# Key and value jobs in turn, eight slots for weights, a second U tile and new scheduler durations in a hybrid attention and DeltaNet layer

## The chip, the core and the metric

One core of a Trainium2 chip runs the whole layer as one program. The metric is the device time of that core in microseconds, from runs of the compiled kernel. The engines are PE (TensorE), DVE (VectorE), ACT (ScalarE), POOL (GpSimd) and SP (SyncE, which issues the DMAs here). All matrices are in float32 at the interface.

## The reference

One decoder layer over 1024 tokens of width 2048, and a final RMSNorm.

```python
h = rms_norm(x, norm_w)
proj = einsum('btd,dc->btc', h, w_in)          # 2048 -> 8208 columns
# group A, 8 heads: differential attention
attn = softmax(q1 k1^T * scale + bias) - lam * softmax(q2 k2^T * scale + bias)
o_da = rms_norm(attn @ v, subln_w) * (1 - lambda_init) * silu(gate)
# group B, 8 heads of 128: gated DeltaNet
q, k, v = silu(causal_depthwise_conv(qkv, conv_w))
o_gdn = gated_delta_rule_chunked(l2norm(q), l2norm(k), v, g, beta)   # chunks of 64
o_gdn = rms_norm(o_gdn, gdn_norm_w) * silu(z)
out = rms_norm(x + concat(o_da, o_gdn) @ w_out, final_norm_w)
```

## The kernel before, in words

**The input projection.** It is cut into jobs. One job makes two blocks of 128 columns for all 1024 tokens, by a scheme with seven products for every four quarter blocks (in the manner of Strassen). Its four quarter weights A11, A12, A21 and A22 are 128 x 1024 float32, 512 KB each, loaded from w_in in rows of 128 columns. Three more operands (S1 to S4, some in place) are sums of these. One product is 24 matmuls of 128x128 by 128x512: eight blocks deep, and three passes, since each float32 operand is split into a float16 value and a float16 remainder (whi and wlo for the weights; B11h, B11l and so on for the activations, made once at the start). There are 32 jobs, in this order (lines 1567 to 1597): four of DeltaNet keys, four of attention values, then for every pair of heads one of gates and two of queries and keys, three of z, eight of DeltaNet queries and values (one per head), and one last of z.

**The weights task** (`weights`, from line 700) runs one step for each product of the job at hand. A step splits one operand (ACT writes whi, then DVE or POOL writes wlo) and does a part of the preparation of the next job: load the four quarters (steps 0 to 3), square each on ACT (steps 1 to 4, each in the step after its load), add the squares up by a small matmul into the PSUM tile `side` (step 5), derive a power-of-two scale for each half, scale the quarters on ACT, and form S1 to S4 on POOL. The raw tiles are a ring of six: one job allocates six slots (A11, A21, S1, A12, A22, S2), so that a quarter of the next job takes the slot of the same quarter of this one.

**Collecting.** Each product is read out of PSUM (two `prod` tiles) and added into the tiles q, U, V and o (`collect`). Of each there is one; only in the second and the fourth job a tile U1 of another pool stands in for U. When a tile is complete, a consumer does what the columns are for. `ev_tile` holds a new use back until the consumers of the last are done.

**What follows.** Each pair of key jobs' heads goes through convolution, Gram matrix and decay (`key_head`), in a lane of its own. After the fourth key job's heads, `inverse` inverts all 128 triangular blocks of 64 on DVE (62 dependent pairs of operations on the tiles tmp and A), merges them on PE, and then starts `attention`: 128 units (8 heads, 8 query blocks, 2 maps). A DeltaNet query or value job's consumer waits for the last head of attention, as it takes over the memory (`head_state`). After the last job and the last scan come 28 groups of four products of the output projection, whose operands are sums and splits made on ACT and on DVE or POOL.

**What sets the order.** Nothing is ordered at run time. `Planner` (from line 175) holds lanes, each a list of generators of instructions; again and again it issues the instruction or DMA that could start earliest by its own clock, made of `Op.cost`, of the delays in `HOP`, and for DMAs (`start`, line 287) of 0.475 us on the queue, 0.65 us, the bytes over 360 GB/s and 0.8 us until others see it. A `Choice` may go to DVE or POOL, whichever ends first, with a lean. During attention a margin (`plan.margin`) keeps its units in step with the products. On the chip each engine runs its instructions in the order thus written, and waits at the first whose operands are not ready. All of them are recorded on line 273, and DMAs on 303, so the rows are told apart by tile names.

Of the kernel before, what the change touches and what calls it, by code (L numbers as in the profile page):

```python
# [23 lines left out]
D = 2048  # L24
H = 8
# [99 lines left out]
class Choice:  # L125
    """The same computation on either of two engines, the second preferred by so many microseconds."""
# [14 lines left out]
class Copy:  # L141
    """A DMA that is still to be issued."""
# [8 lines left out]
class Lane:  # L151
    """Tasks (generators of instructions and conditions) that are issued one after the other."""
# [21 lines left out]

class Planner:
    """Orders the instructions of several lanes by an estimate of when each can start."""

    def __init__(self, tc, lanes):
        self.tc, self.nc = tc, tc.nc
        self.free = dict(pe=0.0, act=0.0, dve=0.0, pool=0.0, queue=0.0, dma=0.0)  # L180
# [6 lines left out]
        self.now = 0.0  # L187
        self.margin = lambda: 0.8
# [98 lines left out]
    def start(self, d):  # L287
# [8 lines left out]
        size = free_len(d.out) * d.out.shape[0] * 4  # L296
# [3 lines left out]
        self.wr[o] = {"dma": max(t1 + 0.8, self.wr.get(o, {}).get("dma", 0.0))}  # L300
        rd = self.rd.setdefault(i, {})
        rd["dma"] = max(t1 + 0.8, rd.get("dma", 0.0))
# [36 lines left out]
class Pool:  # L339
    """A tile pool whose slots the planner follows."""  # L340
# [29 lines left out]
def hybrid_trunk(ctx: ExitStack, tc: tile.TileContext, a, out):  # L370
# [275 lines left out]
    # (operands of the narrow product, the rows of its weights, the column group of the sum)  # L646
# [52 lines left out]

    def weights():  # L700
        cur = None
        for j in range(len(jobs) + 1):
            nxt = {"j": j} if j < len(jobs) else None
            cols = jobs[j][0] if nxt is not None else None

            def load(n):
                c, g = {"A11": (0, 0), "A12": (0, 1), "A21": (1, 0), "A22": (1, 1)}[n]
                t = nxt[n] = wp.tile([P, NH, P], F32, "raw", 6)
                dma(t, w_v[:, g * NH:(g + 1) * NH, cols[c]:cols[c] + P])

            def square(n, k):
                return act.activation(junk(D // 2).rearrange("p (a c) -> p a c", a=NH), nxt[n], AF.Square,
                                      accum_out=nxt["ssq"][:, k:k + 1])
# [3 lines left out]

            def wsplit(st, idx):
                g = 7 * st["j"] + idx
                yield lambda: issued[0] >= g - 2  # L720
                n = ORDER[idx][0]
                hi = wp.tile([P, NH, P], F16, "whi", 3)
                lo = wp.tile([P, NH, P], F16, "wlo", 3)
                yield act.activation(hi, st[n], AF.Copy)
                yield Choice(*(e.tensor_tensor(out=lo, in0=st[n], in1=hi, op=ALU.subtract) for e in (dve, pool)),
                             lean=0.7)
                ready_w[g] = hi, lo
# [5 lines left out]
            if j == 0:  # L733
                yield when("loads")
            for i in range(7):
                if cur is not None and i < 5:
                    yield from wsplit(cur, i + 2)
                if nxt is None:
                    continue
                if i == 0:  # L740
                    nxt["ssq"] = wp.tile([P, 4], F32, "ssq", 2)
                    load("A11")
                elif i == 1:
                    load("A21")
                    yield square("A11", 0)
                elif i == 2:
                    nxt["S1"] = wp.tile([P, NH, P], F32, "raw", 6)
                    load("A12")
                    yield square("A21", 2)
                elif i == 3:  # L750
                    load("A22")
                    yield square("A12", 1)
                elif i == 4:
                    yield square("A22", 3)
                elif i == 5:
# [22 lines left out]
                    s2 = nxt["S2"] = wp.tile([P, NH, P], F32, "raw", 6)  # L778
                    yield either(out=s2, in0=nxt["S1"], in1=nxt["A11"], op=ALU.subtract)
# [3 lines left out]
                else:  # L783
# [7 lines left out]

    def ev_tile(name):
        flags = users.get(name, [])
        yield lambda: all(flags)
        users[name] = []
        return box["kp" if name == "U1" else "ev"].tile([P, 512 + HALO], F32, name)

    def consume(name, task):
        flags = users[name]
# [43 lines left out]
    def collect(j, idx, pt):  # L843
        conv, sink = jobs[j][1:3]
        u, back = state[j]["u"], state[j]["back"]
        over = "U1" if j in (1, 3) else "U"
# [20 lines left out]
        if idx == 1:  # L867
            U = acc_["U"] = yield from ev_tile(over)
# [35 lines left out]
        else:  # L904
            yield add(U, U)
            drained[0] += 1
            consume(over, sink(0, 1, U))

# [670 lines left out]
    for h in range(0, H, 2):  # L1579
# [23 lines left out]
    # (left blocks and their operation, right blocks and theirs, output quarters that take the product)  # L1603
# [147 lines left out]
    def first_halves():  # L1751
        """The squares of the rows' first halves, and these times the last norm's weights."""
# [97 lines left out]
```

## Time and profile before

| | us |
|---|---|
| median of 3 runs | 2399.9 |
| lowest and highest run | 2394.6, 2416.65 |
| span of the profiled execution | 2387.7 |
| its time outside the span | not listed; the median is 12.2 above the span |

The profile is of one execution. Busy times of PE are of pipelined matmuls, so their shares say little about how near PE is to its peak. "Waits" name the releaser that came last. The tile names are those of the program: raw (weights as loaded, and S1 to S4), whi and wlo (their split), jkw (where squares are written, their sum being what is wanted), side (a PSUM tile shared by transposes and the squares' sum), prod (products in PSUM).

### The profile page before, as it was taken

To read this page: it belongs to the slowest core of one execution; us is meant where nothing else is said; L and a number is where in the kernel's file an instruction comes from. 1 tells how busy PE (TensorE), PEld (TensorE's weight loads), DVE (VectorE), ACT (ScalarE), POOL (GpSimd) and SP (SyncE) were. 2 spreads that over 40 slices of the span, in tenths; PEclk is the share of its full clock that TensorE was granted. 3 is DMA by queue.
4 is the path that set the end of the run, shared out by engine and by line. 5 is a ranking of instruction groups with operands and counts; after the bars stand their busy time and mean duration, and the time that the engine had idled before them with its cause. 6 is when DMAs were issued, how large, how long until landed. Compare 5 with 4: busy or idle time off the path is not lost.

```text
span 2387.7 us, 29240 instructions
## 1 busy us (share of the span) xinstructions
PE 1985.4 (83%) x10029; PEld 1201.5 (50%) x10029; DVE 1755.1 (74%) x2841; ACT 1211.8 (51%) x2506; POOL 1033.0 (43%) x696
## 2 busy tenths in 40 slices
PE   3778886788798879788888889978888998899986
PEld 2534443333355445444455445445555556677765
DVE  6868875999628657566677675666666768899998
ACT  6645553343346546555555555645555654333344
POOL 5633552433322322332233223424433436687885
PEclk7898998999899999899999999989999999999998
DMA  6253446332664554544445454234443444613303
GB/s 192 43 117 102 117 133 158 90 101 74 153 163 115 141 118 110 116 120 122 101 126 150 94 103 73 71 86 86 72 83 85 98 131 153 223 62 108 108 33 141
DMA packets 287044, 267.12 MB, mean 112 GB/s; under 512 B 51552, under 2 KB 225840, under 8 KB 285488
## 3 DMA queue, kind: packets, MB, share of 16 engines
q1 hardware_dynamic: 286896, 265.26, 43.6%
q8 instruction: 79, 1.29, 0.2%
q14 instruction: 69, 0.57, 0.1%
HBM read 189.66 MB, written 77.12 MB: 112 GB/s over the span
## 4 chain that ended last, share of the span: by engine, by line
DVE 34%; PE 25%; DMA 22%; ACT 7%; issue 5%; SPq 3%; POOL 3%; POOLq 0%; ACTq 0%; DVEq 0%
PE prod L273 17%; DMA raw<-in_w_in_dram 16%; PE bank L273 5%; DVE wlo L273 5%; SPq L303 3%; DVE tmp L273 3%; DVE acc L273 2%; DVE qT L273 2%; DVE A L273 2%; PE av L273 2%; PE side L273 2%; ACT jkw L273 2%; DVE whi L273 2%; DVE raw L273 1%; DVE c L273 1%
## 5 line engine op out<-in xcount | busy, mean ns | idle before, releaser
L273 PEld LDWEIGHTS <-whi 128*128 128x128 f16 x3680 | 366.7, 102 | 405.0 <-issue 85.8
L273 POOL TENSOR_TENSOR raw<-raw 128x1024 f32<-128x1024 f32 x127 | 324.1, 2559 | 126.3 <-ACT raw L273 71.6
L273 POOL TENSOR_TENSOR wlo<-raw,whi 128x1024 f16<-128x1024 f32 x78 | 183.3, 2350 | 396.2 <-ACT whi L273 384.2
L273 ACT ACTIVATE whi<-raw 128x1024 f16<-128x1024 f32 x224 | 235.0, 1050 | 106.9 <-PE prod L273 91.8
L273 PEld LDWEIGHTS <-wlo 128*128 128x128 f16 x1840 | 187.7, 102 | 198.1 <-issue 29.4
L273 ACT ACTIVATE jkw<-raw 128x1024 bf16<-128x1024 f32 x134 | 141.1, 1053 | 282.4 <-DMA raw<-in_w_in_dram 281.2
L273 DVE TENSOR_TENSOR wlo<-raw,whi 128x1024 f16<-128x1024 f32 x146 | 217.1, 1488 | 51.3 <-ACT whi L273 50.3
L273 PE MATMUL bank<-kst,qst 128*128 128x512 f32 (+3 forms) x384 | 123.6, 423 | 43.7 <-DMA kst<-kdl 19.1
L273 ACT ACTIVATE raw<-raw,sc 128x1024 f32<-128x1024 f32 x128 | 143.0, 1140 | 24.3 <-DVE sc L273 24.3
L273 PE MATMUL prod<-B21h,whi 128*128 128x512 f16 x256 | 107.0, 418 | 11.2 <-DVE V L273 11.2
L273 PE MATMUL prod<-T2h,whi 128*128 128x512 f16 (+1 forms) x280 | 104.0, 375 | 14.3 <-ACT whi L273 11.9
L273 DVE TENSOR_REDUCE nm<-bank 128x1 f32<-128x512 f32 (+2 forms) x192 | 106.6, 555 | 10.7 <-ACT prob L273 4.5
L273 PE MATMUL prod<-T2h,wlo 128*128 128x512 f16 (+1 forms) x280 | 104.3, 376 | 7.8 <-DVE wlo L273 7.8
L273 PE MATMUL prod<-T1h,whi 128*128 128x512 f16 x256 | 103.7, 405 | 6.0 <-DVE U L273 6.0
L273 PE MATMUL prod<-B21l,whi 128*128 128x512 f16 x256 | 107.7, 421 | 0.0
L273 PE MATMUL prod<-B21h,wlo 128*128 128x512 f16 x256 | 107.3, 419 | 0.0
L273 PEld LDWEIGHTS bank<-kst,qst 128*128 128x128 f32 x384 | 71.9, 208 | 66.4 <-ACT prob L273 21.0
L273 PE MATMUL prod<-T1h,wlo 128*128 128x512 f16 x256 | 103.9, 406 | 0.0
L273 PE MATMUL prod<-T2l,whi 128*128 128x512 f16 (+1 forms) x280 | 103.6, 374 | 0.0
L273 PE MATMUL prod<-T1l,whi 128*128 128x512 f16 x256 | 103.4, 404 | 0.0
L273 PE MATMUL prod<-B11h,whi 128*128 128x512 f16 (+1 forms) x280 | 101.4, 366 | 2.0 <-DVE V L273 2.0
L273 PE MATMUL prod<-B11h,wlo 128*128 128x512 f16 (+1 forms) x280 | 101.0, 365 | 2.2 <-POOL wlo L273 2.2
(458 smaller groups left out, 5477.1 us busy)
## 6 DMA issues: line engine op xcount, KB each, us to landing
raw<-in_w_in_dram SPq DMA_DIRECT2D x128, 512.0 KB, 8.8
qst<-qd SPq DMA_DIRECT2D x256, 64.0 KB, 3.2
xt<-in_x_dram SPq DMA_DIRECT2D x8, 1024.0 KB, 9.5
qd<-c SPq DMA_DIRECT2D x32, 256.0 KB, 3.5
B11h<-mixed SPq DMA_DIRECT2D x5, 1024.0 KB, 7.9
T2h<-in_w_out_dram SPq DMA_DIRECT2D x5, 1024.0 KB, 7.4
e<-grow SPq DMA_DIRECT2D x8, 512.0 KB, 10.4
kd<-y SPq DMA_DIRECT2D x8, 512.0 KB, 6.0
```

The lines of the kernel that those rows point to most:

```text
L273: op.fn(*op.args, **op.kw)
L303: self.nc.sync.dma_start(out=d.out, in_=d.in_)
```

## The change

The order of the jobs: the loop that made four key jobs and the loop that made four value jobs become one, so that a value job follows each key job. `weights` allocates and loads by a ring of eight slots, each in the fixed order A11, A21, S1, A12, A22, S2: eight at the start, then one after each split of the current job's last five operands and one in step 5. Squares are taken in steps 0 to 3. U has two tiles for all jobs, and U1 is gone; `ev_tile` looks at the use that is as many back as there are tiles. The first rows of x for the output take the eight slots too. In the scheduler, the time of a transfer follows from its runs of contiguous bytes, POOL operations and some of DVE's exclude each other, and PE's durations follow a model of its clock. The scratch for dynamic DMAs is set to 1024.

```diff
+LAND = 0.8
+def transfer(d):
+    size = free_len(d.out) * d.out.shape[0] * 4
+    runs = [run_dram(v) if v.space == DRAM else run_of(v) for v in (d.out, d.in_)]
+    run = min(min(runs), 16384)
+    packets = size / run
+    each = 0.004 + run / 25.5e3
+    if d.in_.name.startswith('in_w_in') and run <= 512:
+        each = 0.09
+    elif run <= 512:
+        each *= 1.3
+    return max(packets * each / 16, 0.05)
+def ported(op):
+    sb = [v for v in op.aps if v.space != PSUM and free_len(v) > 1]
+    if op.eng == "pool":
+        return op.name not in ("memset", "affine_select")
+    if op.eng != "dve":
+        return False
+    if op.name in ("tensor_tensor", "scalar_tensor_tensor"):
+        return len(sb) > 1
+    return op.name in ("tensor_copy", "tensor_scalar") and bool(sb) and op.out.space != PSUM
...
     def ready(self, op):
-        return max(self.free[op.eng], self.due(op))
+        t = max(self.free[op.eng], self.due(op))
+        if t < INF and ported(op):
+            t = max(t, self.free["port"])
+        return t
...
-        t1 = t0 + op.cost()
+        t1 = self.clock.run(t0, op.cost()) if op.eng == "pe" else t0 + op.cost()
         self.free[op.eng] = t1
+        if ported(op):
+            self.free["port"] = t1
...
-        t1 = max(t0 + q + 0.65, self.free["dma"]) + max(size / 360e3, 0.05)
+        t1 = max(t0 + q + 0.65, self.free["dma"]) + transfer(d)
...
+    RAWS = 8
     def weights():
...
+        def room(j, n):
+            st = state_of(j)
+            if st is None:
+                return
+            t = st[n] = wp.tile([P, NH, P], F32, "raw", RAWS)
+            if n[0] == "A":
...
+                dma(t, w_v[:, g * NH:(g + 1) * NH, c0:c0 + P])
+        RING = ("A11", "A21", "S1", "A12", "A22", "S2")
...
+        yield when("loads")
+        advance(RAWS)
...
             for i in range(7):
                 if cur is not None and i < 5:
                     yield from wsplit(cur, i + 2)
+                    advance()
...
                 if i == 0:
                     nxt["ssq"] = wp.tile([P, 4], F32, "ssq", 2)
-                    load("A11")
+                    yield square(nxt, "A11", 0)
                 elif i == 1:
-                    load("A21")
-                    yield square("A11", 0)
+                    yield square(nxt, "A21", 2)
                 elif i == 2:
-                    nxt["S1"] = wp.tile([P, NH, P], F32, "raw", 6)
-                    load("A12")
-                    yield square("A21", 2)
+                    yield square(nxt, "A12", 1)
                 elif i == 3:
-                    load("A22")
-                    yield square("A12", 1)
-                elif i == 4:
-                    yield square("A22", 3)
+                    yield square(nxt, "A22", 3)
...
-                    s2 = nxt["S2"] = wp.tile([P, NH, P], F32, "raw", 6)
...
+                    advance()
                     yield scaled("A12", 0)
...
+    EV = {"q": 1, "U": 2, "V": 1, "o": 1}
     def ev_tile(name):
-        flags = users.get(name, [])
-        yield lambda: all(flags)
-        users[name] = []
-        return box["kp" if name == "U1" else "ev"].tile([P, 512 + HALO], F32, name)
+        history, bufs = users.setdefault(name, []), EV[name]
+        yield lambda: len(history) < bufs or all(history[-bufs])
+        history.append([])
+        return box["ev"].tile([P, 512 + HALO], F32, name, bufs)
...
     for h in range(0, H, 2):
         pair(5120, h, lambda c, hf, X, h=h: key_conv(h + c, hf, X), True)
-    for h in range(0, H, 2):
         pair(2048, h, lambda c, hf, X, h=h: v_half(h + c, hf, X))
...
-                    acc_load(wp, "raw", 6, 0, tb, (0,))
+                    acc_load(wp, "raw", RAWS, 0, tb, (0,))
...
-    nc = bacc.Bacc("TRN2", target_bir_lowering=False, num_devices=1)
+    nc = bacc.Bacc("TRN2", target_bir_lowering=False, num_devices=1, dynamic_dma_scratch_size=1024)
```

## Rows read from the trace of the kernel before

**Rows 1.** The page's first line and its table of busy times.

```profile
span 2387.7 us, 29240 instructions
...
PE 1985.4 (83%) x10029; PEld 1201.5 (50%) x10029; DVE 1755.1 (74%) x2841; ACT 1211.8 (51%) x2506; POOL 1033.0 (43%) x696
```

**Rows 2.** The page's chain that ended last: shares of the span by line.

```profile
PE prod L273 17%; DMA raw<-in_w_in_dram 16%; PE bank L273 5%; DVE wlo L273 5%; SPq L303 3%; DVE tmp L273 3%; DVE acc L273 2%; DVE qT L273 2%; DVE A L273 2%; PE av L273 2%; PE side L273 2%; ACT jkw L273 2%; DVE whi L273 2%; DVE raw L273 1%; DVE c L273 1%
```

**Rows 3.** Waits, whole span: engine, line <- releaser: us in total, times, longest.

```profile
ACT jkw L273 <- DMA raw<-in_w_in_dram: 281.2, 75, 12.1
...
PE side L273 <- ACT jkw L273: 67.6, 14, 8.8
...
DVE bank L273 <- DMA bias<-bvec: 36.8, 7, 9.1
...
DVE U L273 <- DMA qd<-U: 5.5, 1, 5.5
```

**Rows 4.** Windows, prod: length, PE, PEld, DVE, ACT busy (count), clock, DMA, GB/s.

```profile
131.00:300.00 169.00, 123.06 (x509) 0.00 (x0) 15.38 (x21) 2.01 (x3) 0.91 0.48 119
300.00:517.00 217.00, 160.51 (x673) 0.00 (x0) 20.48 (x28) 2.68 (x4) 0.90 0.47 124
517.00:691.00 174.00, 122.69 (x506) 0.00 (x0) 15.40 (x21) 2.03 (x3) 0.91 0.45 116
691.00:1458.00 767.00, 505.52 (x2018) 0.00 (x0) 61.66 (x84) 8.11 (x12) 0.94 0.50 119
1458.00:1938.00 480.00, 352.45 (x1345) 0.00 (x0) 41.68 (x56) 5.34 (x8) 0.94 0.41 81
```

**Rows 5.** Instructions on the raw tiles: ns min/median/max, starts; last, DMA issue to landing.

```profile
L273 DVE TENSOR_TENSOR wlo<-raw,whi x146: 1203/1225/3390, 75.0 to 1960.9; 128x1024 f16<-128x1024 f32 x146
...
L273 POOL TENSOR_TENSOR wlo<-raw,whi x78: 2119/2133/4036, 54.8 to 1967.9; 128x1024 f16<-128x1024 f32 x78
L273 DVE TENSOR_TENSOR raw<-raw,prod x48: 673/676/689, 1996.8 to 2271.6; 128x512 f32<-128x512 f32 x48
...
DMA to landing us min/median/max: 2.6/8.8/19.3
```

**Rows 6.** Timeline of ACT, 207 to 220 us: start, us, operation, [idle before <-releaser].

```profile
209.65 1.04 ACT L273 ACTIVATE whi<-raw 128x1024 f16<-128x1024 f32 x1
216.33 1.06 ACT L273 ACTIVATE jkw<-raw 128x1024 bf16<-128x1024 f32 x1 [5.64 <-DMA raw<-in_w_in_dram]
```

**Rows 7.** Timeline of PE, 213.5 to 222 us.

```profile
214.61 0.38 PE L273 MATMUL prod<-T1h,whi 128*128 128x512 f16 x1
214.83 0.38 PE L273 MATMUL prod<-T1l,whi 128*128 128x512 f16 x1
218.78 0.68 PE L273 MATMUL bank<-ident,y 128*128 128x128 f32 x4 [3.57 <-DVE y L273]
...
219.68 0.63 PE L273 MATMUL prod<-T1h,whi 128*128 128x512 f16 x1
220.11 0.63 PE L273 MATMUL prod<-T1l,whi 128*128 128x512 f16 x1
```

**Rows 8.** Chain that ended last, by line: 131 to 517 us, then 691 to 1458.

```profile
by line: DMA raw<-in_w_in_dram 23.8%; PE prod L273 10.6%; DVE tmp L273 9.2%; DVE A L273 7.5%; DVE wlo L273 6.9%; SPq L303 6.1%; issue 5.5%; DVE y L273 3.7%; DVE n L273 3.5%; DMA A<-ad 2.6%; DVE U L273 2.1%; PE bank L273 1.8%; DVE V L273 1.7
...
by line: DMA raw<-in_w_in_dram 22.2%; PE prod L273 18.6%; PE bank L273 5.8%; PE av L273 4.1%; DMA kst<-kdl 4.0%; DVE nm L273 3.8%; issue 3.8%; DVE wlo L273 3.5%; SPq L303 3.4%; DMA mixed<-gt 2.7%; PE side L273 2.6%; DVE cc L273 2.4%; DMA bi
```

**Rows 9.** Instructions on the tile A, 380 to 660 us: its load.

```profile
L303 SPq DMA_DIRECT2D A<-ad x1: 326/326/326, 400.4 to 400.4; - x1
```

**Rows 10.** Windows, all instructions; as rows 4, with POOL before the clock.

```profile
691.00:1458.00 767.00, 654.50 (x3273) 374.07 (x3272) 509.48 (x1030) 432.99 (x979) 222.77 (x187) 0.94 0.50 119
...
1988.00:2388.00 400.00, 342.81 (x1397) 264.00 (x1394) 370.08 (x445) 157.12 (x255) 292.64 (x177) 0.95 0.31 111
```

**Rows 11.** The page's DMA queues: packets, MB, share of 16 engines.

```profile
q1 hardware_dynamic: 286896, 265.26, 43.6%
```

**Rows 12.** Waits, 691 to 1458 us.

```profile
ACT jkw L273 <- DMA raw<-in_w_in_dram: 112.6, 28, 8.4
```

More of the change, by code (lines that the diff above doesn't have):

```diff
@@ L172, in advance, with run_of, run_dram, __init__ @@
         return moved
+LAND = 0.8
+def run_of(ap):
+    n = 1
+    for s, k in reversed(list(ap.ap)[1:]):
+        if k == 1:
+            continue
+        if s != n:
+            break
+        n *= k
+    return 4 * n
+def run_dram(ap):
+    n = 1
+    for s, k in reversed(list(ap.ap)):
+        if k == 1:
+            continue
+        if s != n:
+            break
+        n *= k
+    return 4 * n
+def transfer(d):
[9 more added lines that the diff above has]
+    return max(packets * each / 16, 0.05)
+PORT_1 = ("tensor_copy", "tensor_scalar", "memset")
+def ported(op):
[7 more added lines that the diff above has]
+    return op.name in ("tensor_copy", "tensor_scalar") and bool(sb) and op.out.space != PSUM
+WINDOW = 3.4133
+class Clock:
+    def __init__(self):
+        self.window, self.work, self.half = 0, 0.0, True
+    def to(self, t):
+        while t >= (self.window + 1) * WINDOW:
+            share = self.work / WINDOW
+            self.half = share < (0.8 if self.half else 0.45)
+            self.window, self.work = self.window + 1, 0.0
+    def run(self, t0, cost):
+        self.to(t0)
+        t, left = t0, cost
+        while left > 1e-9:
+            edge = (self.window + 1) * WINDOW
+            rate = 0.5 if self.half else 1.0
+            d = min(left / rate, edge - t)
+            if d <= 1e-9:
+                self.to(edge)
+                t = max(t, edge)
+                continue
+            self.work += d
+            left -= d * rate
+            t += d
+            self.to(t)
+        return t
 class Planner:
@@ L179, in __init__ @@
         self.tc, self.nc = tc, tc.nc
-        self.free = dict(pe=0.0, act=0.0, dve=0.0, pool=0.0, queue=0.0, dma=0.0)
+        self.free = dict(pe=0.0, act=0.0, dve=0.0, pool=0.0, queue=0.0, dma=0.0, port=0.0)
         self.wr, self.rd, self.base, self.after = {}, {}, {}, {}
@@ L187, in __init__ @@
         self.now = 0.0
+        self.clock = Clock()
         self.margin = lambda: 0.8
@@ L295, in start @@
         self.free["queue"] = t0 + q
-        size = free_len(d.out) * d.out.shape[0] * 4
-        t1 = max(t0 + q + 0.65, self.free["dma"]) + max(size / 360e3, 0.05)
+        t1 = max(t0 + q + 0.65, self.free["dma"]) + transfer(d)
         self.free["dma"] = t1
         self.ring = self.ring[1:] + [t1 + 0.9]
-        self.wr[o] = {"dma": max(t1 + 0.8, self.wr.get(o, {}).get("dma", 0.0))}
+        self.wr[o] = {"dma": max(t1 + LAND, self.wr.get(o, {}).get("dma", 0.0))}
         rd = self.rd.setdefault(i, {})
-        rd["dma"] = max(t1 + 0.8, rd.get("dma", 0.0))
+        rd["dma"] = max(t1 + LAND, rd.get("dma", 0.0))
         self.nc.sync.dma_start(out=d.out, in_=d.in_)
@@ L698, in hybrid_trunk, with state_of, advance, square @@
     W_LEAN = 2.0
+    RAWS = 8
     def weights():
+        made = {}
+        def state_of(j):
+            return made.setdefault(j, {"j": j}) if j < len(jobs) else None
+        def room(j, n):
[4 more added lines that the diff above has]
+            if n[0] == "A":
+                c, g = int(n[2]) - 1, int(n[1]) - 1
+                c, g = {"A11": (0, 0), "A12": (0, 1), "A21": (1, 0), "A22": (1, 1)}[n]
+                c0 = jobs[j][0][c]
+                dma(t, w_v[:, g * NH:(g + 1) * NH, c0:c0 + P])
+        RING = ("A11", "A21", "S1", "A12", "A22", "S2")
+        place = [0]
+        def advance(n=1):
+            for _ in range(n):
+                j, k = divmod(place[0], len(RING))
+                place[0] += 1
+                room(j, RING[k])
+        def square(st, n, k):
+            return act.activation(junk(D // 2).rearrange("p (a c) -> p a c", a=NH), st[n], AF.Square,
+                                  accum_out=st["ssq"][:, k:k + 1])
+        def wsplit(st, idx):
+            g = 7 * st["j"] + idx
+            yield lambda: issued[0] >= g - 2
+            n = ORDER[idx][0]
+            hi = wp.tile([P, NH, P], F16, "whi", 3)
+            lo = wp.tile([P, NH, P], F16, "wlo", 3)
+            yield act.activation(hi, st[n], AF.Copy)
+            yield Choice(*(e.tensor_tensor(out=lo, in0=st[n], in1=hi, op=ALU.subtract) for e in (dve, pool)),
+                         lean=0.7)
+            ready_w[g] = hi, lo
+        yield when("loads")
+        advance(RAWS)
@@ L701, in weights @@
         cur = None
         for j in range(len(jobs) + 1):
[L703 to L713, printed above, removed]
+            nxt = state_of(j)
@@ L715, in scaled @@
             def scaled(n, c):
                 return act.activation(nxt[n], nxt[n], AF.Copy, scale=nxt["s"][:, c:c + 1])
[L718 to L727, printed above, removed]
@@ L777, in weights @@
                     yield either(out=nxt["S1"], in0=nxt["A21"], in1=nxt["A22"], op=ALU.add)
-                    s2 = nxt["S2"] = wp.tile([P, NH, P], F32, "raw", 6)
-                    yield either(out=s2, in0=nxt["S1"], in1=nxt["A11"], op=ALU.subtract)
+                    yield either(out=nxt["S2"], in0=nxt["S1"], in1=nxt["A11"], op=ALU.subtract)
                     nxt["S3"] = nxt["A21"]
                     yield either(out=nxt["S3"], in0=nxt["A11"], in1=nxt["A21"], op=ALU.subtract)
+                    advance()
                     yield scaled("A12", 0)
-                else:
+                elif i == 6:
                     yield from wsplit(nxt, 1)
@@ L867, in collect @@
         if idx == 1:
-            U = acc_["U"] = yield from ev_tile(over)
+            U = acc_["U"] = yield from ev_tile("U")
             yield add(U, q)
@@ L906, in collect @@
             drained[0] += 1
-            consume(over, sink(0, 1, U))
+            consume("U", sink(0, 1, U))
     Gc = small("Gc", [P, H, NT])
```

6 lines of the change are left out of this document (2 added, 4 removed).

## The prediction

> **What bounds the kernel now.** I read the page's busy table first [rows 1]: no engine is full. PE shows 83% and DVE 74%, and the page warns that a busy PE is not PE at its peak, so the loss has to be found as waiting. The chain that ended last says where it is [rows 2]: beside PE's own products at 17%, the largest entry is the load of input weights into the raw tiles, 16% of 2387.7 us, some 380 us. The view of waits gives the same thing seen from ACT [rows 3]: ACT stood 281.2 us, 75 times, with a sum of squares at its head that wanted a raw tile still in flight; and PE stood 67.6 us at the small matmul that adds up these squares.
>
> The reason is in the code and in the landing times. Before the change a raw tile is loaded in one step of the weights task and squared in the next. One step is one product. From 131 to 1938 us there are 30 jobs [rows 4] (509, 673, 506, 2018 and 1345 matmuls at 168 a job give 3, 4, 3, 12 and 8), so a product takes 1807/210 = 8.6 us on average. The load lands after 8.8 us at the median and 19.3 at worst [rows 5]. Lead and landing are equal: every second load comes late (75 of 128). The old scheduler prices such a load at 512 KB / 360 GB/s = 1.5 us, plus some 1.9 us of fixed terms, so it places the square early and sees no harm in it.
>
> One stall in full [rows 6, 7]: ACT ends a weight copy at 210.7 and stands until 216.33. Behind the square in ACT's queue are the tanh and the copies of the key convolution, so DVE's next step is late, and PE, which has keys' transposes at its head, issues nothing between 214.83 and 218.78. [...]
>
> **The change part by part**, against the profiled execution (its span is 2387.7 us; no time around the span is listed for it, and the median of the runs, 2399.9, lies 12.2 above, which I add at the end).
>
> *A. Ring of eight, loads earlier.* A11 and A21 of the next job are now loaded four steps before their squares, A12 and A22 two steps. Two steps are 17 us at today's pace and 13 to 14 at a pace of 7 us; less the 2 us or so that the slot's last reader takes, that covers the median landing of 8.8 with 3 us to spare, not the tail of 19.3. No instruction and no byte is added: still 128 loads and six slots per job. Saving, bounded below: the 67.6 us that PE itself stood at the squares' sum; above: the 281.2 us of ACT's waiting (the chain's 380 hold SP's issue and landing that another path would partly replace). What ACT does late is not always wanted at once: whi has three buffers. I take 67.6 plus four tenths of the other 213.6, **-153 us**, clock included. The stage where the cover is thinnest is attention, where the load has 22% of the chain [rows 8], 170 us; the least is won while the triangular inversion runs, whose steps on DVE already have 17% of the chain from 131 to 517 [rows 8] (tmp and A).
>
> *B. Second U.* The four-quarter sum U is read by a consumer while the next job's second product wants the tile. The waits show DVE at U standing for a store out of it once, 5.5 us [rows 3]. Bounds 0 and -20 (a few stalls hidden as PE waiting for its accumulator); I take **-5**. The tile U1 it replaces only served the second and fourth job.
>
> *C. Key and value jobs in turn.* The same eight jobs in another order. The keys' heads get a value job's time between two key jobs, but the last key job is the seventh, not the fourth. Now the fourth ends at 300 and the inversion's operand is loaded at 400.4 [rows 9], 100 us later, since the heads' chains run behind. At 49 us a job, the seventh ends at 131 + 6 x 49 = 425; with a lag of 30 to 100 the inversion starts at 455 to 525, and attention, 290 us behind it as now, at 745 to 815 rather than 691. Some 9 jobs then lie beside attention rather than 12. PE's work is unchanged; the stage is denser. Bounds: 0, if attention simply goes faster as its planner's margin asks, and +124 if it keeps its 6.0 us per unit (767/128) from the later start. DVE is busy 509 of 767 us there [rows 10], so there is room; I take **+20**.
>
> *D. Other durations.* The scheduler now prices a raw load at 1024 x 0.09/16 = 5.8 us, close to the measured landing with its fixed terms; it treats POOL operations and DVE operations with two SBUF inputs as exclusive; it models PE's clock. The trace bears out the second: DVE's weight remainder takes 1.20 us at the least and 3.39 at most, POOL's 2.1 to 4.0, while a DVE addition out of PSUM always takes 0.67 to 0.69 [rows 5]. It matters most in the output projection: in its 400 us DVE is busy 370 and POOL 293 [rows 10], and these include waiting for each other. Some operations there may run on either; of a remainder of 1024 elements DVE's least is 0.9 us below POOL's [rows 5], so moving 40 of half that size from POOL to DVE frees the pair by some 18 us. Against it: the leans and margins stay as they are while the durations they are weighed against change, and any new order can put an instruction ahead of one that is urgent. Bounds -50 and +60 (the size of PE's present stall at the squares, if new waits of that kind appear); I take **-20**.
>
> [...]
>
> *E. Start.* Eight slots are asked for at once, so six loads are issued where one was; two of them are the next job's. They share the DMA engines with x. Bounds -5 and +18 (two landings of 8.8); I take 0, as PE waits for the norm of x there. The smaller scratch setting moves nothing: 265 of the 267 MB go through one queue, SP's [rows 11].
>
> Sum: -153 - 5 + 20 - 20 = -158; 2387.7 - 158 + 12.2 = 2242 us.
>
> **The rivals.**
> 1. *DVE takes over.* Loads no longer stall ACT, but DVE, at 74% and full during the inversion and the output projection, ends the next wait. Then only PE's own stand at the squares is won: -68, with C and D cancelling: 2332. For it: DVE operations make up a third of the chain from 131 to 517 [rows 8] (tmp, A, wlo, y, n, U and V). Against: outside those two stages DVE is at two thirds.
> 2. *Larger.* With loads early and ordered well, the ceiling is reached: -281, C +20: 2139. [...] Against: ACT's waits were spread over work that was not all urgent.
> 3. *Slower: attention starts late and binds.* If its chain (scores, minimum, exponential, transposes) and its small loads keep 6.0 us per unit, then from a start at 780 it ends at 1547, 89 after 1458; the DeltaNet heads cannot start before it, and their jobs win back 30: 2387.7 + 59 + 12.2 = 2459. For it: key and bias loads of attention hold 36.8 us of DVE's waiting [rows 3], and 4% of that stage's chain is kst alone [rows 8]. Against: ACT's waits for raw tiles in this stage, 112.6 us [rows 12], hold up attention's exponentials as well. It decides from (1458 - 780)/128 = 5.3 us per unit upward.
> 4. *No change.* New order, new waits of the same size, most likely on SP's queue, which is served in order: 2400.
>
> **How the numbers follow.** Forecast 0.45, DVE 0.25, larger 0.14, slower 0.10, no change 0.06. The first three are all faster by more than 1% (which is about what a measurement of this kernel tells from no change): 0.84. Within 1%: 0.06. Slower: 0.10. The range must leave out no more than a fifth: from just under the larger rival, 2130, to no change, 2400. The forecast's own range, from half the gain of A to all of it, is 2170 to 2310.
>
> **What would show it.** Right: ACT's waiting for raw tiles falls from 281 to under 80 us and the load leaves the top of the chain; PE's stand at the squares nearly goes; the granted clock of the job stages rises to 0.95 or more; a job of the first eight takes under 50 us; the inversion's operand is loaded between 455 and 525; attention takes under 5.3 us per unit; the output projection takes 380 to 395 us. Wrong: ACT's waits fall and the span does not (rival 1 or 4: look at what PE waits for at its first matmul of a product); DeltaNet's first job ends well after 1458 (rival 3); the loads still land late (the two steps were shorter than 9 us, or SP's queue held them back).

## The result, and the profile after

The changed kernel takes 2325.0 us (median of 4 runs, 2323.9 to 2332.5) beside 2397.9 for the kernel before on the same chip: a ratio of 0.970, 95% interval 0.966 to 0.975. It is faster by 3%, 73 us. The forecast was a gain of 158 us. Its range, 2130 to 2400, holds the time, but the gain is less than half of the forecast one, and the rival "DVE takes over" (2332) came nearest, though not by its mechanism. The spans of the two profiles differ by 64 us and not by 73, since the profiled execution of before is 12 us short of its median and that of after 1 us.

The page of the kernel after, its first line, busy times and chain by line:

```profile
span 2324.2 us, 29237 instructions
...
PE 1994.4 (86%) x10029; PEld 1227.5 (53%) x10029; DVE 1647.9 (71%) x2862; ACT 1218.7 (52%) x2516; POOL 912.1 (39%) x665
...
PE prod L367 27%; PE av L367 6%; PE bank L367 6%; DMA raw<-in_w_in_dram 3%; PE side L367 2%; DVE nm L367 2%; SPq L396 1%; ACT jkw L367 1%; DVE wlo L367 1%; DVE al L367 1%; DMA qst<-qd 1%; ACT ah L367 1%; DMA kst<-kdl 1%; DVE prob L367 1%; DVE bank L367 1%
```

The load of raw tiles had 16% of the chain before [rows 2] and has 3% now. But the chain of after could be followed back only to 723 us (its shares add up to some 69% of the span), so the two figures are not of the same stretch. From 723 us to the end alone, the load has 4.2% of the chain after and 13.9% before. The view of waits, whole span, points the same way, against 281.2 and 67.6 us [rows 3]:

```profile
ACT jkw L367 <- DMA raw<-in_w_in_dram: 67.0, 25, 6.9
...
PE side L367 <- ACT jkw L367: 5.3, 5, 2.3
```

The loads themselves did not land sooner. This is their time from issue to landing in the kernel after, 2.6/8.8/19.3 before [rows 5]:

```profile
DMA to landing us min/median/max: 2.6/9.9/22.7
```

They are only asked for earlier. So far all goes as forecast, and the windows (matmuls on prod, columns as in rows 4) show the jobs fast: 1578 matmuls, 9.4 jobs at 168 each, in 382 us are 40.7 us a job, at a granted clock of 1.00.

```profile
131.00:513.00 382.00, 350.11 (x1578) 0.00 (x0) 46.98 (x64) 6.84 (x10) 1.00 0.59 142
513.00:815.00 302.00, 268.79 (x1163) 0.00 (x0) 35.92 (x49) 4.13 (x6) 0.94 0.48 115
815.00:1172.00 357.00, 279.76 (x1181) 0.00 (x0) 35.99 (x49) 4.72 (x7) 0.98 0.56 128
1172.00:1488.00 316.00, 3.65 (x15) 0.00 (x0) 0.00 (x0) 0.00 (x0) 0.71 0.30 87
```

But the last window shows what the forecast lacked. From 1172 to 1488 us the kernel after issues 15 matmuls of the input projection. Products stop after the second product of the second DeltaNet job (at 1178 us; the third starts at 1495), as the tiles into which they are collected are not free: their consumers wait for the last head of attention (`head_state`). The end of attention is the last addition into gt, before and after (instructions on the tile gt; the last figure of the pair is the start of the last one):

```profile
L273 DVE SCALAR_TENSOR_TENSOR gt<-av,sub_s,gt x32: 469/480/486, 747.8 to 1493.3; 128x256 f32<-128x256 f32 x32
```

```profile
L367 DVE SCALAR_TENSOR_TENSOR gt<-av,sub_s,gt x32: 472/484/485, 955.2 to 1487.6; 128x256 f32<-128x256 f32 x32
```

1493.3 and 1487.6 us: all that the jobs won ahead of this point was 6 us at its end. What follows the end, in windows of all instructions, DeltaNet jobs and then output projection, before and after:

```profile
1494.00:1992.00 498.00, 431.03 (x2301) 269.54 (x2300) 332.93 (x606) 276.30 (x678) 204.72 (x142) 0.95 0.43 96
1992.00:2388.00 396.00, 339.76 (x1380) 262.11 (x1379) 366.39 (x441) 153.62 (x247) 288.72 (x175) 0.95 0.31 112
```

```profile
1488.00:1899.00 411.00, 387.21 (x2160) 245.06 (x2161) 293.51 (x595) 257.22 (x644) 154.82 (x117) 0.97 0.48 110
1899.00:2324.00 425.00, 349.88 (x1408) 276.89 (x1407) 335.67 (x457) 158.99 (x262) 260.38 (x172) 0.89 0.30 105
```

So the 64 us between the spans (2387.7 and 2324.2) are 6 of attention's end, 87 of the DeltaNet stage (498 to 411), less 29 of the output projection (396 to 425).

Attention itself began late. The inversion's tile A is loaded at 492 us, in the stretch of 455 to 525 that was forecast (400.4 before, [rows 9]), and stored here at 788.4, while the kernel before stored it at 627.0. First the kernel after, then the one before:

```profile
L396 SPq DMA_DIRECT2D A<-ad x1: 491/491/491, 492.0 to 492.0; - x1
...
L396 SPq DMA_DIRECT2D ud<-A x1: 339/339/339, 788.4 to 788.4; - x1
```

```profile
L303 SPq DMA_DIRECT2D ud<-A x1: 320/320/320, 627.0 to 627.0; - x1
```

From the load of A to the first matmul of attention's scores it took 390 us rather than the 296 of before; the first starts are 882.4 and 695.9:

```profile
L367 PE MATMUL bank<-kst,qst x384: 273/450/796, 882.4 to 1468.4; 128*128 128x512 f32 x96, 128*128 128x128 f32 x32, 128*128 128x256 f32 x32, 128*128 128x384 f32 x32
```

```profile
L273 PE MATMUL bank<-kst,qst x384: 272/397/988, 695.9 to 1464.0; 128*128 128x512 f32 x96, 128*128 128x128 f32 x32, 128*128 128x256 f32 x32, 128*128 128x384 f32 x32
```

Attention caught up once the products had stopped. Its pairs of units, counted by POOL's one operation on l for each pair (POOL's column is the second), are 22 in 290 us beside products and 42 in 316 us alone, 13.2 and 7.5 us a pair; before it was 64 in 798, 12.5 us.

```profile
882.00:1172.00 290.00, 2.89 (x10) 6.25 (x22) 0.98 0.55 123
1172.00:1488.00 316.00, 3.48 (x22) 8.17 (x42) 0.71 0.30 87
```

### The profile page after: what moved, and what is told of

It is laid out like the page before. It is cut to its first block, busy times and chain, and to the rows that moved or that the text cites. A ratio compares the mean times of both kernels' runs of the same rounds, so it can differ in the third digit from the quotient of the medians.

```text
span 2324.2 us, 29237 instructions
## 1 busy us (share of the span) xinstructions
PE 1994.4 (86%) x10029; PEld 1227.5 (53%) x10029; DVE 1647.9 (71%) x2862; ACT 1218.7 (52%) x2516; POOL 912.1 (39%) x665
## 4 chain that ended last, share of the span: by engine, by line
PE 41%; DVE 9%; DMA 6%; ACT 5%; POOL 3%; issue 3%; SPq 1%; ACTq 0%; DVEq 0%; POOLq 0%
PE prod L367 27%; PE av L367 6%; PE bank L367 6%; DMA raw<-in_w_in_dram 3%; PE side L367 2%; DVE nm L367 2%; SPq L396 1%; ACT jkw L367 1%; DVE wlo L367 1%; DVE al L367 1%; DMA qst<-qd 1%; ACT ah L367 1%; DMA kst<-kdl 1%; DVE prob L367 1%; DVE bank L367 1%
## 5 line engine op out<-in xcount | busy, mean ns | idle before, releaser
L367 DVE TENSOR_TENSOR wlo<-raw,whi 128x1024 f16<-128x1024 f32 x181 | 257.5, 1426 | 136.9 <-ACT whi L367 133.9
L367 PE MATMUL bank<-kst,qst 128*128 128x512 f32 (+3 forms) x384 | 142.9, 478 | 60.4 <-DMA kst<-kdl 28.7
L367 POOL TENSOR_TENSOR wlo<-raw,whi 128x1024 f16<-128x1024 f32 x43 | 96.6, 2247 | 227.1 <-ACT whi L367 174.4
L367 PEld LDWEIGHTS bank<-kst,qst 128*128 128x128 f32 x384 | 81.7, 249 | 82.1 <-issue 32.2
L367 PE MATMUL prod<-B21h,whi 128*128 128x512 f16 x256 | 99.2, 387 | 8.3 <-DVE V L367 8.3
L367 PE MATMUL prod<-B11l,whi 128*128 128x512 f16 (+1 forms) x280 | 103.4, 370 | 0.0
L367 PE MATMUL prod<-T3h,whi 128*128 128x512 f16 x256 | 99.3, 388 | 2.6 <-ACT q L367 2.6
L367 PE MATMUL side<-ident,prob 128*128 128x128 f32 x288 | 64.1, 336 | 41.5 <-DVE prob L367 36.4
L367 PE MATMUL prod<-T3l,whi 128*128 128x512 f16 x256 | 99.4, 388 | 0.0
L367 PE MATMUL prod<-B21h,wlo 128*128 128x512 f16 x256 | 99.3, 388 | 0.0
```

## The experiments

All times are medians of four or more runs, each with the kernel before beside it on the same chip; the ratio is to that kernel, with its 95% interval. The kernel before moves from one set of runs to the next (medians of 2386 to 2417), so kernels of different sets are compared by the stages of their profiles as well. That spread need not be the chips': the run with a fixed margin below, whose PE and POOL do the same instructions in the same order as in the changed kernel, took 2327.1 us in another set, 2 us more. "Attention's end" is the last addition into gt; the DeltaNet stage runs from there to the last product of the input projection.

| kernel | us | ratio | A loaded, attention from, to | DeltaNet stage | output |
|---|---|---|---|---|---|
| before | 2397.9 | 1 | 400, 696, 1494 | 498 | 396 |
| changed | 2325.0 | 0.970 | 492, 882, 1488 | 411 | 425 |
| ring only | 2342.2 | 0.979 | 381, 681, 1447 | 493 | 398 |
| durations only | 2436.6 | 1.020 | 443, 759, 1527 | 492 | 430 |
| changed, old durations | 2393.9 | 1.003 | 494, 821, 1525 | 469 | 395 |
| changed, keys first | 2293.6 | 0.959 | 414, 786, 1452 | 409 | 425 |
| changed, one U | 2386.1 | 0.989 | 467, 867, 1483 | 468 | 430 |
| changed, no exclusion | 2361.9 | 0.988 | 478, 803, 1483 | 478 | 399 |
| changed, products held back | 2310.9 | 0.957 | 494, 884, 1463 | 419 | 425 |
| changed, half of attention | 2068.8 | 0.857 | 493, 883, 1242 | 395 | 430 |
| keys first, exclusion in the middle | 2239.9 | 0.934 | 387, 690, 1446 | 399 | 399 |

**The parts of the change.** Keys first, in the changed kernel:

```diff
     for h in range(0, H, 2):
         pair(5120, h, lambda c, hf, X, h=h: key_conv(h + c, hf, X), True)
+    for h in range(0, H, 2):
         pair(2048, h, lambda c, hf, X, h=h: v_half(h + c, hf, X))
```

> The changed kernel with the four key jobs ahead of the four value jobs again. Theory S (the later inversion starts attention late, and products run out beside it: 323 us without a product, 1172 to 1495): the inversion's operand is loaded near 400 us instead of 492, attention has some 100 us more beside products, the stretch without products shrinks from 323 to about 200 us, and the time falls to about 2210 us. Rival H (the order pays, since key heads get a value job's time): the first eight jobs slow from 43 us to 50 or more, and the time is 2325 us or above.

2293.6 us, 0.959 (0.954 to 0.964). Both were half right: the third to the fifth job slow to 61 to 63 us, from 40 to 43, as the rival said, and attention still ends 36 us earlier. The order as changed costs this kernel about 1%.

The old durations in the changed kernel (the added lines of `ready` and `do` and the call of `transfer` taken back):

> The changed kernel with the scheduler's old durations (no exclusion of POOL and DVE, no model of PE's clock, loads at 360 GB/s). Theory P (the new durations hold attention back beside products): attention goes faster beside products, the stretch without products falls below 150 us, and the time below 2260 us. Theory D (the new durations made the jobs fast): jobs of the first stage are back at 50 us or more, ACT waits over 150 us for raw tiles, and the time is 2360 us or more. If the ring of eight did it and the order spoils it, jobs stay under 47 us, the stretch without products stays over 250 us, and the time is 2310 to 2350 us.

2393.9 us, 1.003 (1.000 to 1.005). The time is theory D's, its signs are not: the second to the eighth job take some 48 us instead of 41, ACT waits only 40 us for raw tiles, the stretch without products falls from 317 to some 92 us, and the whole gain is gone, by attention's end (1525) and the DeltaNet stage (469). A short stretch without products is no merit by itself.

The ring alone in the kernel before (its weights task with eight slots):

> The kernel before with the weights task of the ring of eight alone (old order, old durations, old U tiles). Theory R (the loads' lead is what made the jobs fast): ACT waits under 100 us for raw tiles, jobs of the first stage take 46 us, attention starts near 650 us, and the time is 2200 to 2260 us. Theory D (the durations did it): ACT still waits over 150 us, jobs take over 50 us, and the time is above 2340 us.

2342.2 us, 0.979 (0.975 to 0.984). The lead alone takes ACT's waits from 281 to 45 us, so theory R is right on the loads, and brings attention's end forward by 47 us. But the second to the eighth job still take some 53 us (55 before) with the old durations, and the time is above 2340 us, as theory D had these two. Of 236 us of waiting some 50 came out at the end.

The durations alone in the kernel before:

> The kernel before with the new durations of the scheduler alone. Theory D: ACT's waits for raw tiles fall below 120 us and the time to 2300 us or less. Theory R: the lead of one product stays too short, squares are only placed later, ACT's named waits fall but PE waits in their stead, and the time is 2360 to 2400 us.

2436.6 us, 1.020 (1.014 to 1.025): slower, by more than either theory gave. Knowing when a load lands doesn't make it land earlier; its wait for raw tiles is still near that of before (281.2):

```profile
ACT jkw L368 <- DMA raw<-in_w_in_dram: 236.0, 65, 12.9
```

One U tile in the changed kernel:

```diff
-    EV = {"q": 1, "U": 2, "V": 1, "o": 1}
+    EV = {"q": 1, "U": 1, "V": 1, "o": 1}
```

> The changed kernel with one U tile instead of two. If the second U does little (term B, 5 us, and hidden before attention's end): 2320 to 2335 us. If it is what made the jobs of keys and of the DeltaNet heads fast: jobs 1 to 7 take 46 us or more, the last seven jobs over 56 us, and the time is 2350 us or more.

2386.1 us, 0.989 (0.986 to 0.992). The second to the eighth job take some 45 us, the last seven 57 to 65. The span is 57 us longer (2381.0), as much as the DeltaNet stage, 468 us for 411. Between attention's end and the last product PE stood for transposes of a query half whose convolution was late; first with one U, then the changed kernel, last the kernel before:

```profile
PE side L367 <- DVE qT L367: 56.2, 9, 12.0
```

```profile
PE side L367 <- DVE qT L367: 10.7, 3, 5.6
```

```profile
PE side L273 <- DVE qT L273: 24.2, 8, 4.0
```

**Which of the durations.** Without the exclusion (the lines with "port" taken out), without the clock's model (`self.clock.run` replaced by the sum), with a margin of 0.2 for attention, with the old price of loads:

> The changed kernel without the exclusion of POOL and DVE in the scheduler (new load times and PE clock kept). Theory X (the exclusion lengthens the output projection and slows attention beside products): the output projection is back from 425 to some 397 us, attention has done over 30 of its 64 pairs of units when products stop at the 24th job (22 in the changed kernel), and the time falls below 2270 us. Rival C (the PE clock model does both): output 425 us, 22 pairs, 2325 us.

> The changed kernel without the model of PE's clock in the scheduler. Rival C (the clock model holds attention back beside products, as it believes PE slow or busy): over 30 pairs at the stop of products, stretch without products below 230 us, time below 2270 us. Theory X: nothing of this; 22 pairs, output projection 425 us, 2300 to 2350 us.

> The changed kernel with attention's margin fixed at 0.2 us instead of 1.0 or 0.2 by its lead. Theory S (products run ahead because the scheduler lets attention wait up to its margin): attention does more pairs beside products (over 28 at the stop), the stretch without products shrinks by 60 us or more, and the time falls to 2270 us or less. If attention was behind its pace all along, the margin was 0.2 already and nothing moves: 22 pairs, 2325 us.

> The changed kernel with the old price of loads (360 GB/s) and the new exclusion and clock. If knowing the load time made the first jobs fast (41.7 us against 47.8 with all old durations): jobs 1 to 7 take 46 us or more, and ACT's waits for raw tiles rise above 67 us. If the exclusion did that: jobs stay at 42 us. The stop at the 24th job stays above 250 us in either case; time 2310 to 2360 us.

Measured: 2361.9 (0.988, 0.986 to 0.991), 2326.0 (0.973), 2327.1 (0.973) and 2361.6 us (0.987, 0.983 to 0.990). The clock's model leaves the time where it is (output 446 instead of 425 us, the DeltaNet stage and attention's end 10 us less each), and so does the margin: it was at 0.2 already, as the instructions on PE and on POOL are, one for one, those of the changed kernel. The load's price is worth some 1.6%: without it ACT waits 99 us for raw tiles, the second to the eighth job take some 45 us, and attention ends at 1524. The exclusion does three things. It lengthens the output projection (399 without, 425 with; theory X right there). Theory X was right on attention beside products too, with 44 of its pairs done at the stop of products rather than 23, but this brought its end forward by only 5 us, and the time went up. It lengthens the inversion in this kernel: without it A is stored 228 us after its load, with it 296 (in the kernel before the new durations lengthen this only from 227 to 236):

```profile
L392 SPq DMA_DIRECT2D A<-ad x1: 319/319/319, 478.2 to 478.2; - x1
...
L392 SPq DMA_DIRECT2D ud<-A x1: 320/320/320, 706.5 to 706.5; - x1
```

And it shortens the DeltaNet stage, 411 against 478 us, which outweighs the two. The stage is short only with both the exclusion and the second U: 493 with neither (ring only), 468 and 478 with one, 411 with both, each with the ring. What the exclusion does there was not followed further; PE's stand for the query's convolution, 26.1 us without it and 10.7 with it, is a part.

**Does the end of attention set the time?** The products are held to attention's own progress once it has begun:

```diff
-                yield lambda: g in ready_w and drained[0] >= g - 1
+                yield lambda: g in ready_w and drained[0] >= g - 1 and pace[0](g)
...
+        pace[0] = lambda g: g >= start_gdn or (g - first) * len(units) <= (at[0] + 8) * (start_gdn - first)
```

> The changed kernel with the products held back, once attention has begun, to attention's own share of units done (eight units of slack). Theory W: the products before the stop were of no use, as they only ran into the wait for attention; held back, they leave the engines to attention, the stretch without products falls below 80 us, attention ends no later than 1488 (by 1440 if the units beside fewer products come faster than 13 us a pair), and the time is 2270 to 2325 us, not slower. Rival J (products are what the time is made of): delaying them costs what they are delayed, 60 us or more, and the time is 2370 us or above.

2310.9 us, 0.957 (0.954 to 0.961). In the windows of prod, 540 matmuls that the changed kernel did before 1172 us come after it (641 for 1181), the first DeltaNet job begins at 1401 instead of 1113 us, and the span is 17 us shorter, since attention ends 25 us earlier:

```profile
815.00:1172.00 357.00, 163.69 (x641) 0.00 (x0) 20.62 (x28) 2.69 (x4) 0.87 0.50 124
1172.00:1463.00 291.00, 137.49 (x526) 0.00 (x0) 15.40 (x21) 2.04 (x3) 0.88 0.42 97
```

Theory W holds in this kernel, the rival J falls. Half of attention left out says it from the other side:

> The changed kernel with half of attention left out: heads 4 to 7 are computed, the output of heads 0 to 3 is zeros. Theory W (attention's end sets the time): attention, 32 pairs instead of 64, ends some 230 us earlier (32 pairs at the 7.1 us they take alone), near 1260, the stretch without products falls from 323 us to under 110, and the time is 2080 to 2120 us. Rival J (the time is made of products and of PE's work): only the left out work of PE is saved, some 85 us by the sum of its matmuls at full clock, and the time is 2230 us or more.

2068.8 us, 0.857 (0.856 to 0.859), a little below what theory W gave: attention ends 246 us earlier and the span is 258 us shorter (2066.5 for 2324.2). The last addition into gt:

```profile
L367 DVE SCALAR_TENSOR_TENSOR gt<-av,sub_s,gt x16: 471/484/485, 931.9 to 1241.5; 128x256 f32<-128x256 f32 x16
```

**What the parts give together.** The exclusion off from the output projection on (a flag that `ready` asks, cleared at its first product):

> The changed kernel, with the exclusion of POOL and DVE taken out of the scheduler from the first product of the output projection on. If the exclusion itself lengthens the output projection: 425 falls to about 398 us, nothing before it moves, and the time is 2297 us (2293 to 2303). If what came before (another state of the tiles or of the scheduler's clock) does: 425 us and 2325.

2306.1 us, 0.961 (0.958 to 0.965), 3 us above the range given. The window of the output projection has 402 us, DVE busier and the clock at 0.95 instead of 0.89; nothing ahead of it moved by more than 2 us:

```profile
1901.00:2303.00 402.00, 344.94 (x1406) 264.16 (x1404) 380.09 (x450) 158.19 (x262) 289.78 (x178) 0.95 0.31 112
```

With keys first too, and then the exclusion only between attention's start and the output projection, with keys in turn and keys first:

> Keys first, the exclusion off from the output projection on. If parts add up: 2294 less 28, 2266 us.

> Keys in turn as changed, and the exclusion only from attention's start to the output projection. Attention starts near 803 instead of 882. If its start counts: it ends near 1455 and the time is 2265 to 2285 us. If only the output projection counts: 2297 us.

> Keys first, and the exclusion only from attention's start to the output projection. If the parts add up: attention starts near 691, ends by 1435, then 834 less 28 us: 2230 to 2255 us. If attention goes slower by what it starts earlier (as in the two runs with keys first and no exclusion), it ends at 1435 to 1450 all the same and the time is 2255 to 2270 us.

2278.1 us (0.949, 0.945 to 0.953), 2302.7 us (0.959, 0.956 to 0.962) and 2239.9 us (0.934, 0.930 to 0.937). The first is 12 us above the sum of its parts. In the second attention starts at 804 us, 79 earlier, and ends only 2 us earlier, so nearly all of its gain is the output projection's. The last is the fastest kernel of the study that computes everything, some 3.7% below the changed one. Attention ends at 1446, as the second reading had it; the time is the first one's, as the DeltaNet stage took 399 us and not 411:

```profile
L368 DVE SCALAR_TENSOR_TENSOR gt<-av,sub_s,gt x32: 466/484/486, 740.7 to 1445.8; 128x256 f32<-128x256 f32 x32
```

Three more had keys first: without the exclusion, with the products held back, with both.

> The changed kernel with keys first and without the exclusion of POOL and DVE. Theory W (the end of attention sets the time: keys, inversion, attention, then some 840 us of DeltaNet jobs and output): the inversion is loaded near 400, attention starts near 710 us (300 after, as in the other runs without the exclusion; 370 to 390 with it) and ends near 1410; the output projection takes 399; the time is 2230 to 2270 us. Rival J (the pace of the jobs sets it): jobs slow to 52 us as in the run with keys first, or to 55, and the time is 2340 us or above, no better than without the exclusion alone.

> The changed kernel with keys first and the products held to attention's share. Theory W: attention starts near 786 as with keys first alone and ends by 1420; the time is 2220 to 2285 us (2294 with keys first alone). Rival J: over 2320 us.

> Keys first, no exclusion, products held to attention's share. Theory W: attention from 710 to 1350 or so, the output projection 399 us, time 2170 to 2230 us. Rival J: over 2320 us.

2308.6 (0.956), 2328.7 (0.964) and 2310.9 us (0.956): all three miss the gain that theory W gave, and the second is where the rival J had it. In the two without the exclusion the DeltaNet stage takes 481 and 483 us. With the new load price and two U tiles, an attention that starts at 690 ends at 1431 to 1446, one from 786 or 791 at 1452 or 1464 (1480 held back), one from 804 at 1483 or 1486, one from 882 at 1488 (1463 held back). A start some 100 us earlier brings the end forward by some 5 to 35 us: an early attention shares the engines with more products and goes at 11.6 us a pair. The end of attention sets the time, but its start sets the end only in part. Held back by my rule, the products of the keys-first kernel even made attention end later (1480 for 1452). Up to 1300 us it had done 47 pairs held back and 45 not; from there to 1400 it did 15 pairs alone where the products had run out, and 9 where held back ones still ran beside it. So what the rule cost here seems to be the stretch in which attention is alone; this was not tested further.

## Why the prediction was wrong

*The step that failed is the price of term A*, "67.6 plus four tenths of the other 213.6, -153 us". Term A's signs came true: ACT's waits under 80 us (67.0), PE's stand at the squares nearly gone (5.3), jobs of the first eight under 50 us (some 41), and, but for the stretch of the inversion (0.94), a clock over 0.95 while products run (1.00, 0.98, and 0.97 in the DeltaNet stage). "Clock included" has no figure of its own in that price, and no run separates what the clock adds; measured are the granted clocks just given, beside 0.90 to 0.94 before [rows 4]. What was wrong is that time won at the jobs was taken for time won at the end. What else might end last stands in the rivals and not in the sum. The chain of before charged the load with 16%, but that chain runs through products and weights beside another one: keys, inversion, attention. In the kernel before the two arrive together, the second DeltaNet job beginning at 1458 us and attention ending at 1494, with no stop of products between. Once the loads were early, the second was what ended last. The run with products held back shows it: products put off by up to 290 us cost nothing in the changed kernel. Alone, in the kernel before, the ring gave 2.1%, some 50 us, 47 of them at attention's end. In the changed kernel attention's end is only 6 us earlier, and with keys first 42: most of what the ring won there the new order took back.

*Term B* was taken as -5 with bounds 0 and -20. Taken back, it costs 57 us of span. The row it rested on, one wait of 5.5 us for a store out of U, showed the smallest part; the stalls stood under other names, as PE waiting for the query's convolution (24.2 us before). Nor is the 57 U's alone: with the old durations the DeltaNet stage is 493 us with one U (ring only) and 469 with two.

*Term C*, +20 with bounds 0 and +124: the order costs 38 us of span (2324.2 for 2285.8) and 31 by the medians, inside its bounds and 11 to 18 above the value taken. Its working failed in one place: "attention, 290 us behind" the inversion's load was 390 us in the changed kernel, and 325 without the exclusion, where the inversion itself took 228 us and not 296. So most of the difference is the scheduler's exclusion of DVE and POOL while faster products run.

*Term D*, -20 with bounds -50 and +60: its argument stood in the output projection, and there the sign was wrong, +23 us (425 for 402, the run that takes the exclusion out there alone). It counted on 40 operations moving from POOL to DVE; POOL's went from 175 to 172. The scheduler with the exclusion held operations back rather than shifting them: DVE's busy time in the stage fell from 366 of 396 us to 336 of 425, and PE's clock from 0.95 to 0.89. As a whole the new durations are worth -65 us of span in the changed kernel (2389.2 with the old ones) and, in the kernel before, +61 by the profiled execution (2448.6, the slowest of its four; 2.0% by the medians, some 48 us): a planner's constants have no value of their own.

*Term E*, 0 with bounds -5 and +18: the first job's last product ends at 135 us instead of 132.

*The sum.* Taken apart one by one the terms are -50 (ring on the kernel before), -57, +38 and -65 (each taken out of the changed kernel), together -134 us of span, where the change gives -64. They don't add, because up to attention's end they pull at the same limit, and in the DeltaNet stage two of them work only together: that stage has 87 us of the gain, of which the ring alone gave 5 (498 to 493), and B, one of the two, had been put at 5. That the time lies within the range is in part luck.

*The rivals.* Attention late and binding had its place right (products stop for it) and its point wrong: a unit took 4.7 us (606/128), under the 5.3 from which it was to cost time, as it did 42 of its 64 pairs in the 316 us after products had stopped. Its sign was wrong for the same reason. It also took 1458, where the second DeltaNet job begins, for attention's end before, which is 1494. "DVE takes over" gave the right number for a reason that doesn't hold: DVE's share fell to 71%.

*DVE beside POOL.* Of DVE's 146 weight remainders in the kernel before, each with two inputs in SBUF, the 79 beside which POOL ran nothing took 1203 to 1227 ns. The 67 beside which it ran something took 1208 to 3390, half of them no more than 1226. The longest, 3390, began 0.44 us after an addition of POOL's and ended 1.1 us after its end. In the output projection of before, DVE's additions and subtractions of two such inputs, on 128x512, took 677 to 693 ns where POOL ran nothing beside them, and up to 2874 where it did. The runs show that planning with an exclusion of the two is not neutral: it moves three stages by 23, 67 and 68 us, in both directions.

## What to carry to other kernels

Before a stall is priced, find the other chains that run beside the one it is on, and measure how far behind they end; the gain stops where the second one starts to bind. The test is cheap: hold the faster work back, and if the time stays, its speed was worth nothing. If the time grows, that says less: the keys-first kernel lost 35 us (2328.7 for 2293.6) when its products were held back. And test a change to a scheduler's constants stage by stage, since the same term can help one stage and hurt two others.

## What the runs showed of the hardware

In the kernel after, PE's granted clock was 0.98 where attention ran beside products and 0.71 where it ran alone, with PE busy 94% and 61%. Attention's score matmuls took 403 ns on average beside products and 521 alone; of the 128x512 form, which is half of them in both, 470 and 600. Groups of instructions, the kernel after, alone (1172 to 1495) and then beside products (882 to 1172):

```profile
L367 PE MATMUL bank<-kst,qst 128*128 128x512 f32 (+3 forms) x244 | 100.5, 521 | 48.6 <-DMA kst<-kdl 22.5 <-DVE prob L367 21.3 <-issue 2.1
```

```profile
L367 PE MATMUL bank<-kst,qst 128*128 128x512 f32 (+3 forms) x140 | 42.4, 403 | 11.8 <-DMA kst<-kdl 6.2 <-DMA qst<-qd 5.5
```

So attention alone, at 7.5 us a pair, ran on a PE with a granted clock of 0.71. That products woven in more thinly keep the clock up was not tested by itself: the changed kernel with products held back had a clock of 0.88 there, and its attention ended 25 us earlier, but which part of that is the clock's was not separated.
